# Second parts of weight tiles made by accumulating DMA instead of VectorE, and a room of its own for one sum

## The chip, the cores and the metric

The kernel runs on one core of one Trainium2 chip. The metric is the device time of one execution in microseconds. TensorE (PE) multiplies matrices, VectorE (DVE) and ScalarE (ACT) work on elements, GpSimd (POOL) does some elementwise work and issues DMAs, SyncE (SP) issues most loads. All matrix products of this kernel are float32 products made of three passes in a reduced float32 form ("fp32r"): every operand is split into a first part `hi`, the operand rounded to that form, and a second part `lo`, what the rounding left; the product is hi·hi + hi·lo + lo·hi.

## The reference

Two layers over 512 tokens of width 1024. Each layer is a half SwiGLU block, a mixing block, and another half SwiGLU block:

```python
x = x + 0.5 * swiglu(rms_norm(x, ffn1_norm[l]), ffn1_wg[l], ffn1_wu[l], ffn1_wd[l])
h = rms_norm(x, mix_norm[l])
z = h @ w_in[l]                       # 1024 x 2304: q | k | v | conv_B | conv_C | conv_h
attn_out = sliding_window_attention(q, k, v, attn_sink[l])   # 8 heads of 64, 2 of keys
conv_out = short_conv(z[B], z[C], z[H], conv_w[l])           # B * conv3(C * H), 3 taps
x = x + jnp.concatenate([attn_out, conv_out], axis=-1) @ w_out[l]
x = x + 0.5 * swiglu(rms_norm(x, ffn2_norm[l]), ffn2_wg[l], ffn2_wu[l], ffn2_wd[l])
```

A final RMS norm follows. The change is in the mixing block: the projection `h @ w_in` and the one by `w_out`.

## The kernel before

Activations are held transposed, with features on the 128 partitions and the 512 tokens along the row. Weights come from HBM in tiles of 128 x 1024 float32 values (512 KB).

**The stream of weight tiles.** `plan` writes the whole list of weight tiles (`order`) ahead of time, in the order in which TensorE takes them. For each it notes how the second part is made. `need_raw` loads tiles up to four ahead into eight buffers (`stock`, tag "raw"), by SP; a tile that is a sum of two weight blocks gets its second block by an accumulating DMA from POOL on top of the first (L193). The same eight buffers hold the attention's probabilities `p` and the values `vv`. `need_split` makes the two parts two tiles ahead, in three buffers each (`wh`, `wl`). There are two ways. `split` (L198, L199) lets ScalarE copy the tile to `hi` and VectorE subtract to get `lo`. `split_far` (L203 to L205) lets ScalarE write the negative of the tile, rounded, into `lo` and the copy into `hi`, and then an accumulating DMA issued by POOL adds the tile to `lo`. What `order` says is "far" goes the second way, all else the first.

**The input projection.** 18 tiles per layer, in the order of `MIX_COLS` (two tiles for each entry): keys, values, four tiles of queries, then for each half of the convolution's channels two tiles of C, two of H, two of B. `group` multiplies one tile with all 512 tokens: 24 matmuls of 512 columns, 5.4 us. Between the groups `mix` puts the attention, eight blocks (4 blocks of tokens by 2 groups of heads), each in three steps that `attend` spreads over the groups: `scores` (L1166, L1167; maxima and exponentials on VectorE and ScalarE, L1170 to L1195), `turn` (TensorE transposes the probabilities, L1202; ScalarE and VectorE split them, L1205 and L1206), and `values` (L1216, L1217; the result goes to `mixed[0]` by L1219 and L1222). The convolution of a channel tile is: product C·H on POOL (L1259), two scalings on ScalarE (L1261, L1263), one tap on VectorE (L1264), the sum on POOL (L1267), and the product with B into `mixed[1]` on POOL, or on VectorE for the last (L1274).

**The output projection.** `share` computes it by a scheme of seven products of quarter blocks in place of eight. The seven weight operands are named in `FORMS`: a11, a12, s2, s3, s1, a22, s4, each in two halves; s1 and s3 are the tiles loaded with an accumulating DMA, s2 and s4 are sums made in place (L223, L246). The seven activation operands are made by `Seven.make` from the four quarters b11, b12, b21, b22 of `mixed`: b11, b21 and b22 themselves, and t3 = b12 - b22, t2 = t3 - b11, t1 = b11 - b12, t4 = t2 + b21. All are split into two parts; t1, t4 and b22 by `split_far`. The sums t3 and t2 have a room of their own (`room_g8`); t1 is written over b12 and so has to come after t3:

```python
if what == "t1":
    nc.vector.tensor_sub(b12, b11, b12)
```

In the output projection the tile a11's first half gets its second part by `split_far`, the others by `split`.

**What orders the work.** A scheduler orders each engine's instructions when the program is built, outside of the stretch that is fixed by hand at the start. On the chip every engine works through its own list in order and waits by semaphores. A pool with n buffers makes a new tile wait until the oldest one's readers are done. A DMA's readers and writers are done when it has landed.

In trace names, `x_m`, `w_m`, `y_m` are the output projection's sums, `fb11h_m` and `fb11l_m` the parts of b11 (`ft2l_m`: second part of t2), `acc` the input projection's sums, `cb`, `cc`, `ch` the scaled convolution tiles B, C, H.

Of the kernel before, what the change touches and what calls it, by code (L numbers as in the profile page):

```python
# [8 lines left out]
F32 = mybir.dt.float32  # L9
# [6 lines left out]
P = 128  # L16
# [7 lines left out]
KC = D // P  # L24
# [3 lines left out]
H = S // 2  # L28
# [30 lines left out]
def trunk_kernel(  # L59
# [23 lines left out]
    nc = tc.nc  # L83
# [14 lines left out]
    def g8(name, dt=F32R, shape=(P, 2, 2, S)):  # L98
        return work.tile(list(shape), dt, tag="g8", bufs=4, name=name)
# [9 lines left out]
    def form(name, dt=F32R, shape=(P, KC // 2, H)):  # L109
        return xpool.tile(list(shape), dt, tag="xf", bufs=14, name=name)  # L110
# [57 lines left out]
    order = []  # L168
# [3 lines left out]
    def add_unit(*unit):  # L172
        units.append(unit)
        return len(units) - 1
# [109 lines left out]
    def abreast(kc):  # L284

        return max(1, KC // kc) if kc in (2, 4) else 1
# [10 lines left out]
    def plan():  # L297
        def cols(src, k0, kc, n, how=None):
            wide = abreast(kc)
            for b in range(0, n, wide):  # L300
                order.append((add_unit((src, k0, kc, b * P, wide * P)), how))

        def plain(wg, wu, b):
            for w in (wg, wu):
                for j in range(2):
                    order.append((add_unit((w, 0, KC, (2 * b + j) * P, P)), None))

        def up(wg, wu, b):
            top, low = ((w, k, KC // 2, 2 * b * P, 2 * P) for w, k in ((wu, 0), (wu, KC // 2)))
            first = (wg, 0, KC // 2, 2 * b * P, 2 * P)  # L310
            u = add_unit(first)
            add_unit((wg, KC // 2, KC // 2, 2 * b * P, 2 * P))
            add_unit(top, low)
            add_unit(top, first)
            add_unit(low)
            order.extend((u, what) for what in FORMS)

        def seven(at, how):


            u = len(units)
            for what in (((0, 0),), ((1, 0), (1, 1)), ((0, 1),), ((1, 0), (0, 0)), ((1, 1),)):
                for h in range(2):
                    add_unit(*(at(o, j, h) for o, j in what))
            order.extend((u, (what, h, how(what, h))) for what in FORMS for h in range(2))

        def ffn(wg, wu, wd, stages):
            for what, b in stages:
                how = "far" if b == (0,) and stages is not FIRST else None
                if what == "p":  # L330
                    plain(wg, wu, b)
                if what == "u":
                    up(wg, wu, b)
                if what == "w":
                    seven(
                        lambda o, j, h: ((wg, wu)[o], KC // 2 * j + 2 * h, 2, 2 * b * P, S),
                        lambda what, h: "far" if (b, what, h) == (1, "a11", 0) else None,
                    )
                if what == "s":
                    seven(  # L340
                        lambda o, j, h: (wd, 2 * b + KC // 2 * j + 2 * h, 2, o * S, S),
                        lambda what, h: "share",
                    )
                if what != "d":
                    continue
                if stages is not LAST or b[-1] < FF // (2 * P) - 1:
                    cols(wd, 2 * b[0], 2 * len(b), KC, how)
                    continue
                for half in range(2):
                    for k in range(0, 2 * len(b), 2):  # L350
                        u = add_unit((wd, 2 * b[0] + k, 2, half * S, S))
                        if half == 0:
                            order.append((u, "wide"))

        for l in range(DEPTH):
            ffn(ffn1_wg[l], ffn1_wu[l], ffn1_wd[l], INNER if l else FIRST)
            for c in MIX_COLS:
                for j in range(2):
                    order.append((add_unit((w_in[l], 0, KC, (2 * c + j) * P, P)), None))
            seven(  # L360
                lambda o, j, h: (w_out[l], KC // 2 * j + 2 * h, 2, o * S, S),
                lambda what, h: "far" if (what, h) == ("a11", 0) else "share",
            )
            ffn(ffn2_wg[l], ffn2_wu[l], ffn2_wd[l], INNER if l + 1 < DEPTH else LAST)


    MIX_COLS = (2, 0, 1, 5, 7, 3, 6, 8, 4)
    plan()


# [12 lines left out]
    class Norm:  # L383
        def __init__(self, i):
            self.i = i
            self.h = [None] * KC
            self.acc = None
            self.inv = None
            self.pairs = {}
            self.begun = set()  # L390
            self.order = range(KC)
# [100 lines left out]
    class Seven:  # L492

        def __init__(self, full, room, name, far=()):
            self.full, self.room, self.name, self.forms = full, room, name, {}
            self.far = far

        def make(self, *names):  # L500
            for what in names:
                if what in self.forms:
                    continue
                hi, lo = (form(f"f{what}{n}_{self.name}") for n in "hl")
                self.forms[what] = (hi, lo)
                b11, b12, b21, b22 = (
                    self.full[j][:, :, t * H : (t + 1) * H] for j in range(2) for t in range(2)
                )
                if what == "t2":
                    self.sums = self.room(self.name)  # L510
                    t3, t2 = self.sums
                    nc.vector.tensor_sub(t3, b12, b22)
                    nc.vector.tensor_sub(t2, t3, b11)
                if what == "t1":
                    nc.vector.tensor_sub(b12, b11, b12)
                if what == "t4":
                    nc.vector.tensor_add(self.sums[1], self.sums[1], b21)
                src = {"b11": b11, "b21": b21, "b22": b22, "t1": b12}.get(what)
                if src is None:
                    src = self.sums[0 if what == "t3" else 1]  # L520
                (split_far if what in self.far else split)(hi, lo, src)

    def room_g8(name):
        t = g8(f"sums_{name}", F32, (P, 2, KC // 2, H))
        return t[:, 0], t[:, 1]

    def room_stock(name):
        return [stock(f"sum{n}_{name}", shape=(P, KC // 2, H)) for n in range(2)]
# [577 lines left out]
    def mix(l, norm, after):  # L1106
        q = [None] * NH

        mixed = [g8(f"m_{l}_{j}", F32, (P, KC // 2, S)) for j in range(2)]
        ops = Seven(mixed, room_g8, f"m_{l}", far=("t1", "t4", "b22"))  # L1110

        def scaled(acc, name, by=None):
            t = g2(name)
# [11 lines left out]
        for g in range(NKV):  # L1125
            own = slice(g * HD, (g + 1) * HD)
# [20 lines left out]
        class Unit:  # L1147


            def __init__(self, n, g):  # L1150
                self.n, self.g = n, g
                self.name = f"{l}_{n}_{g}"
                self.lo = 0 if n else P
# [95 lines left out]
        for pair in range(2):  # L1249
            cs = []  # L1250
            for j in range(2):
                cs.append(scaled(group(norm.h), f"cc_{l}_{pair}_{j}"))
                attend(step)
                step += 1
            ys = []
            for j in range(2):
                c = 2 * pair + j
                u = scaled(group(norm.h), f"ch_{l}_{pair}_{j}")
                nc.gpsimd.tensor_mul(u, u, cs[j])  # L1259
                y = cs[j]  # L1260
                nc.scalar.activation(y, u, AF.Copy, scale=conv_of(l, 2, c))  # L1261
                tap = g2(f"tap_{l}_{c}")
                nc.scalar.activation(tap[:, 1:], u[:, : S - 1], AF.Copy, scale=conv_of(l, 1, c))  # L1263
                nc.vector.scalar_tensor_tensor(  # L1264
                    tap[:, 2:], u[:, : S - 2], conv_of(l, 0, c), tap[:, 2:], op0=ALU.mult, op1=ALU.add
                )
                nc.gpsimd.tensor_add(y[:, 1:], y[:, 1:], tap[:, 1:])  # L1267
                ys.append(y)
                attend(step)
                step += 1  # L1270
            for j in range(2):
                b = scaled(group(norm.h), f"cb_{l}_{pair}_{j}")
                eng = nc.vector if pair and j else nc.gpsimd
                eng.tensor_mul(mixed[1][:, 2 * pair + j, :], b, ys[j])  # L1274
                attend(step)
                step += 1
                if step == 17:
                    ops.make("b11")
        ops.make("b21", "b22")
        share(ops, 1.0, after.step, soon={0: ("t2", "t1"), 1: ("t3", "t4")})  # L1280

    class into:

# [53 lines left out]
```

## Time and profile before

| | us |
|---|---|
| median of 3 runs (lowest, highest) | 1692.32 (1690.91, 1693.9) |
| the profiled execution's own time | 1691.7 |
| its span, from first to last instruction | 1689.9 |
| TensorE busy | 1677.1 (99%) |
| VectorE busy | 1382.9 (82%) |
| ScalarE busy | 967.6 (57%) |
| GpSimd busy | 215.2 (13%) |
| granted TensorE clock | 0.999 |

A busy TensorE is not a TensorE at its peak: matmuls overlap and their ends are modelled, so gaps between them are read from their starts. In a run of 512-column matmuls one starts 0.23 us after the other, though each is shown as 0.39 us long. Layer 0's mixing block lies between about 349 and 513 us of the span, layer 1's between 1184 and 1347. The output projection starts at 470.5 and 1304.8.

### The profile page before, as it was taken

The numbers are of one execution on the slowest core, as the hardware profiler recorded it, in microseconds if no ns is written. First come the engines' busy times: TensorE is split into PE (matmuls) and PEld (weight loads), VectorE is DVE, ScalarE is ACT, GpSimd is POOL, SyncE is SP. The second block draws the span as 40 slices with busy tenths as digits, with TensorE's granted clock in tenths as the row PEclk, the third lists the DMA queues.
The fourth block names the chain that finished last, engine by engine and source line by source line (L and its number), as shares of the span: only waits on it lengthen the run. The fifth ranks groups of instructions, "written<-read, shape, count | busy, mean of one in ns | idle before, by whom it ended". The sixth has DMA issues, their size and how long they took to land.

```text
span 1689.9 us, 23565 instructions
## 1 busy us (share of the span) xinstructions
PE 1677.1 (99%) x9014; PEld 1443.9 (85%) x9014; DVE 1382.9 (82%) x1817; ACT 967.6 (57%) x1335; POOL 215.2 (13%) x192
## 2 busy tenths in 40 slices
PE   9999999999999999999999999999999999999998
PEld 7888899988898888889988888999888978888886
DVE  7987679988799876799798677997787998667995
ACT  6545565466566655564465555644555766556654
POOL 1011111001221111111011111110013111111111
PEclk9999999999999999999999999999999999999999
DMA  8467777731597677778566777884226867777881
GB/s 250 103 171 189 185 198 189 187 100 51 134 215 163 170 191 184 185 194 214 159 145 179 187 185 183 199 213 142 62 63 146 217 136 194 184 184 186 225 212 51
DMA packets 191846, 284.19 MB, mean 168 GB/s; under 512 B 9004, under 2 KB 77684, under 8 KB 191732
## 3 DMA queue, kind: packets, MB, share of 16 engines
q1 hardware_dynamic: 151108, 199.95, 37.4%
q0 software_dynamic: 39472, 81.27, 28.3%
q8 instruction: 71, 1.16, 0.3%
q10 hardware_dynamic: 1152, 1.45, 0.2%
q14 instruction: 43, 0.35, 0.1%
HBM read 261.14 MB, written 2.10 MB: 156 GB/s over the span
## 4 chain that ended last, share of the span: by engine, by line
PE 94%; DVE 2%; DMA 2%; issue 1%; POOL 0%; ACT 0%; POOLq 0%; DVEq 0%; SPq 0%; ACTq 0%
PE x L692 24%; PE y L692 12%; PE x_s L677 8%; PE acc L274 7%; PE acc L271 7%; PE acc L278 7%; PE w L692 6%; PE y_s L677 4%; PE x_s L692 3%; PE w_s L677 2%; PE x_m L677 2%; PE at L898 2%; DMA wl<-raw 2%; PE y_m L677 1%; PE y_s L692 1%
## 5 line engine op out<-in xcount | busy, mean ns | idle before, releaser
L198 ACT CAST wh<-raw 128x1024 fp32r<-128x1024 f32 (+1 forms) x482 | 505.2, 1048 | 536.8 <-PE x L692 133.9
L199 DVE TENSOR_TENSOR wl<-raw,wh 128x1024 fp32r<-128x1024 f32 (+1 forms) x481 | 588.5, 1226 | 206.8 <-ACT wh L198 204.9
L271 PE MATMUL acc<-xh,wh 128*128 128x512 f32 x448 | 176.6, 394 | 0.1
L274 PE MATMUL acc<-xl,wh 128*128 128x512 f32 x448 | 175.4, 392 | 0.1
L278 PE MATMUL acc<-xh,wl 128*128 128x512 f32 x416 | 162.5, 391 | 0.0
L193 POOL DMA_DIRECT2D raw<-in_ffn_wu_dram x39 | 47.2, 1216 | 530.2 <-DVE wl L199 252.7
L274 PEld LDWEIGHTS acc<-xl,wh 128*128 128x128 f32 x448 | 84.2, 188 | 18.5 <-DVE xl L402 1.5
L271 PEld LDWEIGHTS acc<-xh,wh 128*128 128x128 f32 x448 | 84.3, 188 | 17.5 <-ACT xh L401 0.5
L278 PEld LDWEIGHTS acc<-xh,wl 128*128 128x128 f32 x416 | 78.1, 188 | 16.1
L223 DVE TENSOR_TENSOR raw<-raw,raw 128x1024 f32<-128x1024 f32 x58 | 71.0, 1229 | 9.2 <-DMA wl<-raw 6.9
L193 POOL DMA_DIRECT2D raw<-in_ffn_wg_dram x39 | 47.3, 1249 | 229.2 <-DMA raw<-in_ffn_wu_dram 97.2
L193 POOL DMA_DIRECT2D raw<-in_ffn_wd_dram x32 | 38.6, 1210 | 259.4 <-DMA raw<-in_ffn_wd_dram 133.4
L692 PE MATMUL w<-wh,fb21h 128*128 128x512 f32 x152 | 60.7, 399 | 0.0
L692 PE MATMUL x<-wh,ft2h 128*128 128x512 f32 x152 | 60.6, 398 | 0.0
L692 PE MATMUL y<-wh,ft3h 128*128 128x512 f32 x152 | 60.4, 398 | 0.0
L692 PE MATMUL x<-wl,fb11h 128*128 128x512 f32 x152 | 59.3, 390 | 0.4 <-DMA wl<-raw 0.4
L692 PE MATMUL w<-wl,fb21h 128*128 128x512 f32 x152 | 59.4, 391 | 0.0
L692 PE MATMUL x<-wl,ft2h 128*128 128x512 f32 x152 | 59.3, 390 | 0.0
L692 PE MATMUL y<-wh,ft3l 128*128 128x512 f32 x152 | 59.2, 390 | 0.0
L692 PE MATMUL y<-wl,ft3h 128*128 128x512 f32 x152 | 59.2, 390 | 0.0
L692 PE MATMUL w<-wh,fb21l 128*128 128x512 f32 x152 | 59.2, 389 | 0.0
L692 PE MATMUL x<-wh,fb11l 128*128 128x512 f32 x152 | 59.1, 389 | 0.0
(497 smaller groups left out, 4807.4 us busy)
## 6 DMA issues: line engine op xcount, KB each, us to landing
raw<-in_ffn_wu_dram SPq DMA_DIRECT2D x127, 512.0 KB, 4.2
raw<-in_ffn_wd_dram SPq DMA_DIRECT2D x104, 512.0 KB, 4.9
raw<-in_ffn_wg_dram SPq DMA_DIRECT2D x87, 512.0 KB, 4.9
raw<-in_ffn_wu_dram POOLq DMA_DIRECT2D x39, 512.0 KB, 8.0
raw<-in_ffn_wg_dram POOLq DMA_DIRECT2D x39, 512.0 KB, 5.9
raw<-in_w_in_dram SPq DMA_DIRECT2D x36, 512.0 KB, 3.6
raw<-in_ffn_wd_dram POOLq DMA_DIRECT2D x32, 512.0 KB, 8.1
raw<-raw POOLq DMA_DIRECT2D x20, 512.0 KB, 7.0
```

Of the source, the lines that this page charges most:

```text
L193: nc.gpsimd.dma_start(out=r, in_=rows_of(*more), accum_op=ALU.add)
L198: nc.scalar.copy(hi, raw)
L199: eng.tensor_sub(lo, raw, f32(hi))
L223: nc.vector.tensor_add(a11, a11, s1)
L271: nc.tensor.matmul(acc, hi[:, k, :], rhs[k][0], start=k == first, stop=False)
L274: nc.tensor.matmul(acc, hi[:, k, :], rhs[k][1], start=False, stop=n == 0 and k == last)
L278: nc.tensor.matmul(acc, lo[:, k, :], rhs[k][0], start=False, stop=k == last)
L677: nc.tensor.matmul(accs[c // 2][:, c % 2, :], w[:, k, cols], x_[:, 2 * h + k, :], start=start and c % 2 == 0 and h + k + i == 0, stop=h + ...
L692: nc.tensor.matmul(accs[u], x_[:, 2 * h + k, tok], w[:, k, :], start=start and h + k + i == 0, stop=h + k == 2 and i == 2, skip_group_chec ...
L898: nc.tensor.transpose(tp[:, t * P : (t + 1) * P], ups[t][:, c * P : (c + 1) * P], ident)
```

## The change

Three edits, which act in both layers.

The last four entries of `MIX_COLS` (eight of the 18 tiles: the second channel half of C, H and B and the first half's B) are marked "far", so that their second parts are made by `split_far`. In the order of the stream these are tiles 11 to 18: first half's B, then C, H and B of the second half.

The output projection's first tile (a11, first half) loses the mark and is split by ScalarE and VectorE.

The sum t1 of the output projection gets a buffer of its own (the fourth of the four of tag "g8") instead of b12's place. So it no longer has to follow t3, and is asked for with b11 at step 17, ahead of b21 and b22.

```diff
-            for c in MIX_COLS:
+            for i, c in enumerate(MIX_COLS):
                 for j in range(2):
-                    order.append((add_unit((w_in[l], 0, KC, (2 * c + j) * P, P)), None))
+                    u = add_unit((w_in[l], 0, KC, (2 * c + j) * P, P))
+                    order.append((u, "far" if i >= MIX_FAR else None))
             seven(
                 lambda o, j, h: (w_out[l], KC // 2 * j + 2 * h, 2, o * S, S),
-                lambda what, h: "far" if (what, h) == ("a11", 0) else "share",
+                lambda what, h: "share",
             )
...
     MIX_COLS = (2, 0, 1, 5, 7, 3, 6, 8, 4)
+
+    MIX_FAR = 5
...
-        def __init__(self, full, room, name, far=()):
+        def __init__(self, full, room, name, far=(), own=None):
             self.full, self.room, self.name, self.forms = full, room, name, {}
-            self.far = far
+            self.far, self.own = far, own
...
                 if what == "t1":
-                    nc.vector.tensor_sub(b12, b11, b12)
+                    t1 = self.own(self.name) if self.own else b12
+                    nc.vector.tensor_sub(t1, b11, b12)
...
+    def room_one(name):
+        return g8(f"sum1_{name}", F32, (P, 2, KC // 2, H))[:, 0]
...
-        ops = Seven(mixed, room_g8, f"m_{l}", far=("t1", "t4", "b22"))
+        ops = Seven(mixed, room_g8, f"m_{l}", ("t1", "t4", "b22"), room_one)
...
                 if step == 17:
-                    ops.make("b11")
+                    ops.make("b11", "t1")
         ops.make("b21", "b22")
-        share(ops, 1.0, after.step, soon={0: ("t2", "t1"), 1: ("t3", "t4")})
+        share(ops, 1.0, after.step, soon={0: ("t2",), 1: ("t3", "t4")})
```

More of the change, by code (lines that the diff above doesn't have):

```diff
@@ L514, in make @@
                 if what == "t1":
-                    nc.vector.tensor_sub(b12, b11, b12)
+                    t1 = self.own(self.name) if self.own else b12
+                    nc.vector.tensor_sub(t1, b11, b12)
                 if what == "t4":
                     nc.vector.tensor_add(self.sums[1], self.sums[1], b21)
-                src = {"b11": b11, "b21": b21, "b22": b22, "t1": b12}.get(what)
-                if src is None:
+                src = {"b11": b11, "b21": b21, "b22": b22}.get(what)
+                if what == "t1":
+                    src = t1
+                elif src is None:
                     src = self.sums[0 if what == "t3" else 1]
```

## The prediction, made before the changed kernel was run

> **What bounds the kernel now.** I read the page first, then the stretches of the mixing stage by engine, then who made TensorE wait, then TensorE's and VectorE's rows at those places, and last the chain of waits through the end of layer 0's input projection. The page:
>
> ```profile
> span 1689.9 us, 23565 instructions
> PE 1677.1 (99%) x9014; PEld 1443.9 (85%) x9014; DVE 1382.9 (82%) x1817; ACT 967.6 (57%) x1335; POOL 215.2 (13%) x192
> ...
> PE 94%; DVE 2%; DMA 2%; issue 1%; POOL 0%; ACT 0%; POOLq 0%; DVEq 0%; SPq 0%; ACTq 0%
> ```
>
> TensorE sets the time. An edit that removes none of its instructions can only win the gaps between them. Two stretches of layer 0 (the last input tiles with their attention; the output projection):
>
> ```profile
> 420.00:470.00 50.00, 49.29 (x247) 41.37 (x246) 38.15 (x90) 26.13 (x55) 13.96 (x12) 1.00 0.52 128
> 470.00:513.00 43.00, 41.61 (x341) 41.05 (x341) 42.40 (x59) 30.80 (x42) 7.88 (x7) 1.00 0.90 208
> ```
>
> The columns are PE, PEld, DVE, ACT, POOL busy, granted clock, DMA share, GB/s. The clock is full. VectorE is nearly full from 470 on, ScalarE about half busy, the DMA engines half busy up to 470. The waits of TensorE over the whole run:
>
> ```profile
> PE o L1217 <- DVE pl L1206: 1.4, 2, 0.7
> PE w_m L677 <- DVE fb21l_m L199: 1.3, 2, 0.9
> PE x_m L677 <- DVE wl L199: 1.0, 2, 0.5
> ```
>
> So VectorE makes TensorE late at three places, once in each layer, and all three lie in the stage that is edited. The rows show the size, from start to start:
>
> ```profile
> 456.41 0.39 PE L1216 MATMUL o<-ph,vv 128*128 128x512 f32 x1
> 457.50 0.50 PE L1217 MATMUL o<-pl,vv 128*128 128x512 f32 x1 [0.71 <-DVE pl L1206]
> ...
> 476.27 0.28 PE L677 MATMUL w_m<-fb21h_m,wh 128*128 128x256 f32 x1
> 477.43 0.39 PE L677 MATMUL w_m<-fb21l_m,wh 128*128 128x256 f32 x1 [0.88 <-DVE fb21l_m L199]
> ...
> 483.52 0.28 PE L677 MATMUL x_m<-ft2l_m,wh 128*128 128x256 f32 x1
> 484.31 0.39 PE L677 MATMUL x_m<-ft2h_m,wl 128*128 128x256 f32 x1 [0.51 <-DVE wl L199]
> ```
>
> A 512-column matmul follows its forerunner by 0.23 us, a 256-column one by 0.12. The losses are 0.86 (call it gap 1), 1.04 (gap 2) and 0.67 (gap 3); the same rows of layer 1 give 0.81, 0.57 and 0.66. Layer 0 loses 2.57, layer 1 2.04, together **4.6 us. That is all the change can win** (0.27%). Gap 1 has its cause in VectorE's rows: the split of P18 takes 1.97 us beside a POOL sum and ends just before the part that TensorE waits for.
>
> ```profile
> 454.88 1.97 DVE L199 TENSOR_TENSOR wl<-raw,wh 128x1024 fp32r<-128x1024 f32 x1
> 456.77 0.68 DVE L1206 TENSOR_TENSOR pl<-pt,ph 128x512 fp32r<-128x512 f32 x1
> ```
>
> **The change, part by part (layer 0; layer 1 is the same 834 us later).** I call the 18 tiles of the input projection P1 to P18 and use the order of the built program.
>
> VectorE loses eight splits (P11 to P18), gets back the split of the first tile of the output projection: net seven of 1.14 us (start to start), 8.0 us per layer. Nearly all lie in its slack; only P18's lies on gap 1. With it gone the row at 456.77 can start when ScalarE's copy of the same block is there, at 455.3, and gap 1 goes (0.86). The sum t1 keeps its 1.22 us but moves from behind the second sum to a place before P18's scaling, where VectorE now idles: before, it sat 3.7 us until 467.36 on the landing of the one DMA-made tile, which the change makes by VectorE. So gap 3, where t1 stood ahead of the awaited split, goes (0.67, less than t1's 1.14).
>
> ScalarE gets net seven operations of 0.95 us (start to start of such rows), 6.7 us per layer, mostly in idle time (26.13 busy of 50). They stand ahead of attention copies at three places; the nearest is P18's at about 450.6, in the 1.39 us that it idles before the row at 451.95. Cost nothing; without that idle time it would be up to 0.95 at gap 1.
>
> POOL gets net seven DMA issues of 0.9 us and the DMA engines seven more 512 KB accumulations. Issue to landing of the 17 such transfers is 4.5 to 11.2 us, median 6.8: 6.2 beside one plain load (532), 8.0 at 459.35. P11 to P15 have their tiles 4 to 9 us before TensorE needs them, by 6.8. The cover there is the three-deep buffer of second parts; if it were gone each microsecond would be TensorE's.
>
> The new waits decide. A tile's raw buffer is freed by the landing of its accumulation now, so the first loads of the output projection wait for it on SP, and POOL, which works in order, waits for those loads before it adds to them. Before, the same place reads so in the chain of waits:
>
> ```profile
> 448.34 3.85 DMA raw<-in_w_out_dram
> 452.35 0.86 issue
> 453.21 1.22 POOL raw L193
> ...
> 458.13 1.22 POOL ch L1259
> 459.35 7.99 DMA wl<-raw
> ```
>
> The load is that of the second half of the sum s1, released by P17's split on VectorE. After: ScalarE has P17's negative at 444.4 (P14 ends at 442.3, then two operations), POOL issues at 444.8; landing 6.2 later (one load beside it) 451.0; SP's load 3.85: 455.0; POOL starts 0.9 after it: 455.9, instead of 453.21. Queued behind on POOL: P18's accumulation at 457.0, the convolution sum (1.3, ends 459.2) and the next product (1.3, ends 460.5, instead of 459.41). From that product's end to the last attention part, VectorE's second row of L1206 in that block, took 4.3 us (459.41 to 463.71), so 464.8; TensorE wants it at 464.85 less 0.86 = 464.0. **Late by 0.8**, where there was no gap. P18's part lands at 457.0 + 6.9 = 463.9 (between 6.2 and 7.6), needed at 464.7: in time.
>
> It also holds SP: the load of a12's second half waits for P18's landing, the one of s3 behind it starts at 464.5 and lands at 469.0 (4.5); POOL adds to it from 469.6 for 1.2, and only then makes the convolution product (1.4 to 2.1) that gap 2's operand comes from: 472.5. Then sum t3, a split and that split, 3.5 in all: 476.0; TensorE wants it at 476.27 - 0.86 + 0.12 = 475.5, so late by 0.5. Delays on one engine do not add, the later counts: 0.8 in place of gaps 1 and 2. Bounds of this lateness: 0 when landings take 4.5 (the quickest row), 5.4 when they take 8.0 (below). I take 0.8, as the nearest rows are those beside one load.
>
> The Trainium skill, "DMA: Bandwidth & Descriptors", section "Anatomy of one DMA", prices a POOL-issued DMA at 2.0 us plus bytes over 436 GB/s; 512 KB would take an estimated 3.2 us. By it the lateness would be 0 and the time that of rival A. The trace does not agree: no accumulation lands in under 4.4 us.
>
> Sum: layer 0 wins 2.57 - 0.8 = 1.8, layer 1 2.04 - 0.8 = 1.2, together 3.0. The profiled run took 1691.7 (1689.9 span plus 1.8 around it), 0.6 under the median 1692.3. So 1688.7 for it, **1689.3 us as the median**.
>
> **The rivals.** *A, all gaps go and none comes:* 1692.3 - 4.6 = 1687.7. For it: up to 470 the DMA engines have room, and accumulations with little beside them took 4.5 to 5.5 (862, 1360). Against: in the new order each has a load beside it.
>
> *B, the forecast;* its own range, by lateness 0 to 1.8, is 1688 to 1691.5.
>
> *C, the POOL and SP chain becomes the bound:* accumulations take 8.0 as at 459.35, the s1 load 4.35 (465.27), three loads in a row 6.3 (484.32). Then P17 lands at 452.8, load 457.3, POOL 458.2, P18 issued 459.3, landed 467.3, s3's load 474.2, POOL's product 477.4, gap 2's operand 480.9: late by 5.4. Twice that less 4.6 is +6.2: 1698.5. It turns the sign at a lateness of 2.3 (half of 4.6) and costs over 0.2% from 4.0. For it: every link is in series and shares the 16 engines, whose share from 420 to 470 rises from 0.52 to about 0.8 (28.3% of the span over some 155 POOL transfers is 3.1 us each, five more of them). Against: the loads before 459 landed in 3.8 to 4.3.
>
> The skill's same page, section "Issuing engines are not separate DMA queues", has all queues interleave on the same 16 engines; the rows agree (4.5 with one neighbour, 11.2 with three at 1370).
>
> *D, the edit does not reach the gaps,* since other work takes the freed slots: 1692.3. The order of the built program speaks against it.
>
> **How the numbers follow.** Chances: A 0.25, B 0.40, C 0.30, D 0.05. 0.2% (3.4 us) is about what a measurement of this kernel can tell from no change. Faster by more: A and a quarter of B (lateness under 0.6), 0.34. Within: the rest of B and D, 0.36. Slower: C, 0.30. As both signs hold much, B's own range stands above; mine runs from A less 0.7 (half the runs' spread to a side) to C: 1687.0 to 1699.0.
>
> **What would show it.** Right: no wait of TensorE for VectorE's P18 split, nor at gap 3; a new wait of about 0.8 at the last attention block's product (L1216 and L1217 rows near 464), POOL's accumulating load near 456, P18's landing near 464. A: no TensorE wait over 0.3 us in the stage. C: TensorE waits for a DMA-made tile or, near 477, for over 3 us. Wrong outright: waits before P16, or in other stages.

## The result and the profile after

The changed kernel takes **1695.57 us** (median; 1693.67 to 1698.92), the kernel before 1691.93 (1690.42 to 1693.90): the ratio is 1.0025, 95% interval 1.0019 to 1.0032. It is slower by 3.6 us, where the prediction said faster by 3.0. The profiled execution took 1698.92 (span 1697.0), 3.3 over the median, so what it lost has to be told apart from what every run loses. Lines from `Seven` on stand 9 lower in this kernel: L1206 is now L1215, L1216 and L1217 are L1225 and L1226, L677 is L686.

The page after, then the two stretches that the prediction showed (PE, PEld, DVE, ACT, POOL busy, granted clock, DMA share, GB/s):

```profile
span 1697.0 us, 23595 instructions
PE 1678.1 (99%) x9014; PEld 1444.5 (85%) x9014; DVE 1373.3 (81%) x1803; ACT 980.9 (58%) x1349; POOL 224.3 (13%) x206
...
PE 94%; DVE 2%; DMA 2%; issue 1%; ACT 1%; POOL 0%; SPq 0%; DVEq 0%; POOLq 0%; ACTq 0%
```

```profile
420.00:470.00 50.00, 47.39 (x236) 39.18 (x235) 33.13 (x87) 31.38 (x67) 14.49 (x14) 1.00 0.64 140
470.00:513.00 43.00, 42.02 (x334) 41.12 (x333) 40.86 (x54) 29.64 (x41) 8.55 (x8) 1.00 0.94 233
```

The edit did what it says: 14 VectorE instructions fewer, 14 more on ScalarE and on POOL. From 420 to 470 VectorE has 5 us less to do. TensorE shows 1.9 us less as well, because it stood. Who made TensorE wait (total, times, longest):

```profile
PE x L701 <- DMA wl<-raw: 2.1, 1, 2.1
PE o L1225 <- ACT ph L1214: 2.0, 1, 2.0
PE o L1226 <- DVE pl L1215: 1.8, 2, 1.2
PE pt L1211 <- DVE p L1204: 1.8, 2, 0.9
PE w_m L686 <- DVE fb21l_m L199: 1.6, 2, 1.0
```

Gap 3 is gone, and no attention block before the last waits. Gap 2 (`w_m`) stayed. Two waits are new in the stage: `pt`, once per layer, and the last attention block (`o`). One lies elsewhere: `x` L701, at 885, in layer 1's first half block. TensorE's rows of layer 0 at the three places:

```profile
406.12 0.28 PE L1175 MATMUL sc<-kh,q 128*128 128x256 f32 x1
407.29 0.87 PE L1211 MATMUL pt<-ident,p 128*128 128x128 f32 x6 [0.89 <-DVE p L1204]
...
464.00 0.39 PE L278 MATMUL acc<-xh,wl 128*128 128x512 f32 x1
466.38 0.49 PE L1225 MATMUL o<-ph,vv 128*128 128x512 f32 x1 [1.99 <-ACT ph L1214]
467.49 0.50 PE L1226 MATMUL o<-pl,vv 128*128 128x512 f32 x1 [0.62 <-DVE pl L1215]
...
480.90 0.39 PE L686 MATMUL w_m<-fb21l_m,wh 128*128 128x256 f32 x1 [0.98 <-DVE fb21l_m L199]
```

From start to start, less the usual 0.12 or 0.23, that is 1.05 at 406; 2.14 and 0.88 and two steps of 0.1 near 464, together 3.2; 1.14 at 480. Layer 1 has 1.05, 1.5 and 0.78. So the stage loses 5.4 and 3.3 where it lost 2.57 and 2.04: 4.1 more.

The stages, from TensorE's starts: *A* runs from the layer's first scores to the first `x_m`, *B* from there to the first `x` matmul of the second half block.

| | A, layer 0 | B, layer 0 | A, layer 1 | B, layer 1 | sum against before |
|---|---|---|---|---|---|
| before | 87.25 | 76.37 | 87.20 | 75.87 | |
| after | 90.49 | 75.72 | 88.69 | 75.36 | +3.6 |
| after, a second execution | 91.10 | 74.45 | 90.89 | 74.47 | +4.2 |

The +3.6 is also the difference of the medians. The rest of this execution's +7.1 lies for the most part (+4.05) between layer 0's second half block and layer 1's first scores, with the wait at 885 in it; in the second execution that stretch is as long as before (670.70 against 670.72), and its time was 1695.42. So the loss is made in the mixing stages, and the wait at 885 is there in one execution and not in the other.

### The profile page after: what moved, and what is told of

Its sections match the earlier page's. It is cut to its first block, busy times and chain, and to the rows that moved or that the text cites. A ratio compares the mean times of both kernels' runs of the same rounds, so it can differ in the third digit from the quotient of the medians.

```text
span 1697.0 us, 23595 instructions
## 1 busy us (share of the span) xinstructions
PE 1678.1 (99%) x9014; PEld 1444.5 (85%) x9014; DVE 1373.3 (81%) x1803; ACT 980.9 (58%) x1349; POOL 224.3 (13%) x206
## 3 DMA queue, kind: packets, MB, share of 16 engines
q8 instruction: 71, 1.16, 0.3%
q10 hardware_dynamic: 1152, 1.45, 0.2%
## 4 chain that ended last, share of the span: by engine, by line
PE 94%; DVE 2%; DMA 2%; issue 1%; ACT 1%; POOL 0%; SPq 0%; DVEq 0%; POOLq 0%; ACTq 0%
PE x L701 24%; PE y L701 12%; PE x_s L686 8%; PE acc L274 7%; PE acc L271 7%; PE acc L278 7%; PE w L701 6%; PE y_s L686 4%; PE x_s L701 3%; PE x_m L686 2%; PE w_s L686 2%; PE at L907 2%; PE y_m L686 1%; PE y_s L701 1%; DMA wl<-raw 1%
## 5 line engine op out<-in xcount | busy, mean ns | idle before, releaser
L198 ACT CAST wh<-raw 128x1024 fp32r<-128x1024 f32 (+1 forms) x468 | 490.5, 1048 | 517.7 <-PE x L701 136.1
L199 DVE TENSOR_TENSOR wl<-raw,wh 128x1024 fp32r<-128x1024 f32 (+1 forms) x467 | 571.3, 1225 | 211.0 <-ACT wh L198 209.5
L701 PE MATMUL x<-wl,fb11h 128*128 128x512 f32 x152 | 59.9, 394 | 2.1 <-DMA wl<-raw 2.1
L701 PE MATMUL w<-wh,fb21h 128*128 128x512 f32 x152 | 60.7, 399 | 0.0
L701 PE MATMUL x<-wh,ft2h 128*128 128x512 f32 x152 | 60.6, 398 | 0.0
L701 PE MATMUL y<-wh,ft3h 128*128 128x512 f32 x152 | 60.4, 398 | 0.0
L701 PE MATMUL x<-wh,fb11l 128*128 128x512 f32 x152 | 59.9, 394 | 0.0
L701 PE MATMUL w<-wl,fb21h 128*128 128x512 f32 x152 | 59.4, 391 | 0.0
L701 PE MATMUL x<-wh,fb11h 128*128 128x512 f32 x152 | 59.4, 393 | 0.0
L701 PE MATMUL x<-wl,ft2h 128*128 128x512 f32 x152 | 59.3, 390 | 0.0
L701 PE MATMUL y<-wh,ft3l 128*128 128x512 f32 x152 | 59.2, 390 | 0.0
L701 PE MATMUL y<-wl,ft3h 128*128 128x512 f32 x152 | 59.2, 390 | 0.0
```

Of the source, the lines that this page charges most:

```text
L198: nc.scalar.copy(hi, raw)
L199: eng.tensor_sub(lo, raw, f32(hi))
L701: nc.tensor.matmul(accs[u], x_[:, 2 * h + k, tok], w[:, k, :], start=start and h + k + i == 0, stop=h + k == 2 and i == 2, skip_group_chec ...
```

## The experiments

The edits below are to the line that sets the marks, `order.append((u, "far" if ... else None))`, unless another is shown; tile Pn has `2 * i + j == n - 1`. Each ratio is to the kernel before, run beside it, with its 95% interval. The kernel before had medians from 1691.02 to 1691.93 in these sets of runs, so where two kernels of different sets are compared, the difference is also given by what each is against its own run of before.

### Which part costs

**P11's mark away** (`"far" if 2 * i + j > 10`).

> Changed kernel, but tile P11 is split by VectorE again (P12 to P18 stay far). Built so, TensorE's order has the eight transposes of block (2,0) behind seven matmuls of P10's group again, as before the change. Theory T (two causes: the mark on P11 moves those transposes ahead, about 1.05 us of waiting per layer at the row near 406; the chain of P17 and P18 costs the rest): the wait for the normalised probabilities goes, the wait near 464 stays at 3.2 in layer 0; 1695.6 - 2.1 = 1693.5. Rival R1 (the chain alone): 1695.6. Rival R2 (every accumulation costs alike, 3.6 / 8 = 0.45 each): 1695.1.

1694.35, ratio 1.0018 (1.0009 to 1.0028): 1.2 less than the changed kernel, which alone is within the intervals. The wait for `p` is gone from its trace, as the built order says. The wait at 464, which theory T kept in layer 0, is not in this trace either: here the convolution's earlier product stood behind POOL's accumulating load (451.99), and the attention block before the last waited, four times between 456 and 458, 2.0 in all.

**P17's and P18's marks away** (`"far" if i in (5, 6, 7)`).

> Changed kernel, but tiles P17 and P18 are split by VectorE again (P11 to P16 stay far). TensorE's order is that of the changed kernel. Theory T: the wait near 464 (3.2 in layer 0, 1.5 in layer 1) goes and the wait for VectorE's split of P18 comes back (0.86 and 0.81): 1695.6 - 3.0 = 1692.6; the wait near 406 stays at 1.05. R1: the same 1692.6. R2: 1695.6 - 0.9 = 1694.7, with a wait near 464 still there.

1688.74, ratio 0.9980 (0.9972 to 0.9989): 6.8 less than the changed kernel, more than twice what theory T gave. The marks on these two tiles turn a gain into a loss. Of the stage's waits only the one for `p` is left, 0.9 per layer. Gap 1 did not come back, though VectorE splits P18 again. The split now stands at 454.31, ahead of both rows of L1215, with nothing of POOL beside it:

```profile
454.31 1.21 DVE L199 TENSOR_TENSOR wl<-raw,wh 128x1024 fp32r<-128x1024 f32 x1
```

**Both away** (`"far" if 10 < 2 * i + j < 16`: only P12 to P16).

> Changed kernel, but P11, P17 and P18 are split by VectorE again (only P12 to P16 far). Theory T: neither wait; gap 1 back, gap 3 gone: 1691.9 - 1.3 = 1690.6. R1: also 1690.6 if P11's mark costs nothing, but then the first of these four kernels would not be faster than the changed one. R2: 1695.6 - 1.35 = 1694.2.

1687.62, ratio 0.9976 (0.9967 to 0.9985). Theory T was 3 too high, R1 too (P11's mark does cost: 1.1 here against the one before). R2 fell: five marks gain.

**No mark** (`"far" if i >= 9`), with t1's room and a11 split by VectorE.

> Changed kernel without any far mark: the input tiles are split by VectorE as before, the sum t1 keeps its own room and a11's first half is split by VectorE. Theory T: as the one before, 1690.6, gap 1 present, gap 3 gone. R2: 1695.6 - 3.6 = 1692.0. A third rival, R3 (t1's new place and a11's split on VectorE cost something): above 1692.5.

1689.93, ratio 0.9989 (0.9981 to 0.9998), 0.7 under theory T; R3 fell. So the marks P12 to P16 are worth 2.3; they take gap 1 down (0.86 and 0.62 in this trace, 0.4 and none with them).

### What t1's room and a11's mark do

**t1's room alone** (kernel before, `Seven(..., room_one)`, `ops.make("b11", "t1")`, the new `soon`).

> Kernel before with the sum t1 in its own room, made with b11, and nothing else (no input tile far; a11's first half still far). With a11 split by VectorE as well, it was 1689.93, gaps 2 and 3 gone. Theory V (gap 3 was t1's place, gap 2 was VectorE standing until 467.4 for a11's landing before it may overwrite that tile): gap 2 stays, 1690.6. Rival (t1's place made both gaps): 1689.9, no wait of the w_m rows.

1695.55, ratio 1.0025 (1.0014 to 1.0035): worse than either theory. Gap 2 grew and got a second part:

```profile
PE w_m L686 <- DVE fb21l_m L199: 2.1, 2, 1.1
PE w_m L686 <- ACT fb21h_m L198: 1.3, 2, 0.7
```

With a11 still far, VectorE stands until 466.87, and t1 (1.21, at 471.98) then lies in the backlog, ahead of what gap 2 needs. The stage table gives +2.6 for the profiled execution (the quickest of this kernel's runs); the rest of the 4.5 is not seen in it.

**a11's mark away, alone** (kernel before, `lambda what, h: "share"`).

> Kernel before with the output projection's first tile split by VectorE, and nothing else. t1's room alone was slower than before by 4.5, both together faster by 2. Theory V (VectorE stands until about 467 for that tile's landing before it may overwrite it, all its later work is late by that): gap 2 goes, gap 3 stays or shrinks, 1689 to 1690.6. Rival (the two edits only work together): 1691 to 1692.

1688.96, ratio 0.9979 (0.9970 to 0.9988), no wait at gaps 2 and 3; gap 1 is left (1.4 in two). Theory V holds, and further than said: with VectorE's standing for a11's landing both gaps are gone. In the kernel before it stood 3.7 us there:

```profile
467.36 1.23 DVE L223 TENSOR_TENSOR raw<-raw,raw 128x1024 f32<-128x1024 f32 x1 [3.66 <-DMA wl<-raw]
```

**P12 to P16 without t1's room** (the mark as in the third; t1 as before).

> P12 to P16 far and a11 split by VectorE, but the sum t1 over b12 and after t3, as before the change. The same with t1's room was 1687.62. If t1's room wins gap 3 (0.67 and 0.66): 1688.9. If it wins nothing once VectorE no longer stands for a11's landing: 1687.6.

1687.15, ratio 0.9971 (0.9961 to 0.9981). t1's room brings nothing: without it the time is 0.5 less here and 1.0 less without marks, neither beyond the intervals. **This kernel has the lowest time of all**, 4.6 under its run of before, though the intervals do not tell it from P12 to P16 with t1's room; no wait of the mixing stage in its list is left.

**P12 to P15** (`"far" if 10 < 2 * i + j < 15`, with t1's room).

> Changed kernel with P12 to P15 far only. T1 says of P16 what it says of P17: its landing sets the start of the load under s1's first half. With P12 to P16 far POOL stands 10.9 us for that load, until 449.4, but the convolution's product behind it has its other operand only near then, and no later wait of TensorE follows. So T1: within 0.5 of 1687.62, to either side; with one split more on VectorE, up to 0.4 slower at gap 1.

1687.66, ratio 0.9972 (0.9960 to 0.9983): P16's mark is worth nothing measurable either way.

### Why P17 and P18 cost

**P17 alone, P18 alone**, beside P12 to P16 (`10 < 2 * i + j < 17`; `2 * i + j in (11, 12, 13, 14, 15, 17)`).

> Changed kernel with P12 to P17 far, P11 and P18 split by VectorE. The marks on P17 and P18 together cost 6.7 (1694.35 with both, 1687.62 with neither). Theory T1 (P17's landing sets the start of the load under s1's second half, for which POOL stands still with the convolution's work behind it): most of it comes with P17 alone, 1692 to 1694. Rival R4 (P18's own accumulation, issued late on POOL ahead of the convolution's sums and landing late, is what costs): 1687.6 to 1688.5.

> Changed kernel with P12 to P16 and P18 far, P11 and P17 split by VectorE. T1: the load under s1's second half starts again when VectorE has split P17, as before the change; P18's accumulation adds one issue of about 0.9 on POOL, and P18's split leaves VectorE: 1687 to 1689. R4: 1692 to 1694.

1691.95 (ratio 1.0007, 0.9998 to 1.0015) and 1688.31 (0.9985, 0.9977 to 0.9994). P17 costs most, as T1 says: 4.3 by the times, 5.2 by each kernel's own run of before. P18 alone costs 0.7 or 1.6 in the same way, which the intervals do not tell from nothing; the two together cost 6.7. POOL's rows with P17 far:

```profile
458.06 1.21 POOL L193 DMA_DIRECT2D raw<-in_w_out_dram  x1 [5.47 <-DMA raw<-in_w_out_dram]
458.84 1.74 POOL L1276 TENSOR_TENSOR cc<-cc,tap 128x511 f32<-128x511 f32 x1
460.09 1.74 POOL L1268 TENSOR_TENSOR ch<-ch,cc 128x512 f32<-128x512 f32 x1
```

**A ninth raw buffer** (tag "raw" 9 in place of 8, tag "g2" 12 in place of 14), with P12 to P18, P12 to P16, P12 to P17, and P12 to P16 with P18:

> The kernel of the first experiment (P12 to P18 far), with nine raw buffers in place of eight, so that each tile's load waits for the tile one earlier; for room the pool of 2 KB tiles (g2) has 12 in place of 14. The number of accumulations and their bytes stay. T1: the load under s1's second half waits for P16's landing, which was about 7 us before P17's, and POOL no longer stands still: 1687 to 1689.5, with no wait over 1 us near 456 and 464. R4, or rival R5 (more bytes on the 16 DMA engines slow every transfer): 1694, as with eight buffers.

> The kernel with nine raw buffers and twelve g2 buffers, but with P17 and P18 split by VectorE (P12 to P16 far). With nine buffers and P12 to P18 far it was 1695.29, although its trace shows no wait at 464. T1: with the ninth buffer the marks on P17 and P18 cost little more, so that this kernel is within 1.5 of it, 1693.8 to 1696.5; what is lost there is the price of the ninth buffer and the smaller pool in other stages. R4 and R5 (the accumulations themselves cost): 6.7 less, about 1688.6, as with eight buffers.

> Nine raw buffers, P12 to P17 far. With eight buffers P17's mark cost 4.3. T1 (it costs by the wait for its landing alone): near the nine-buffer kernel without it, 1689 to 1691. If the accumulation itself costs: 1693.5 or more.

> Nine raw buffers, P12 to P16 and P18 far. Theory W (P18's landing holds SP's next loads, POOL stands for s3's base load with the last convolution sum and product behind it, and these stretch VectorE's sums): wait at gap 2 of 1.0 to 1.8 per layer, stage of the attention unchanged; 1692 to 1695. If P17 and P18 cost only together: within 1 of 1689.9.

| nine buffers | time | ratio |
|---|---|---|
| P12 to P16 | 1689.90 | 0.9985 (0.9976 to 0.9995) |
| P12 to P17 | 1700.80 | 1.0057 (1.0045 to 1.0069) |
| P12 to P16 and P18 | 1693.79 | 1.0013 (1.0004 to 1.0022) |
| P12 to P18 | 1695.29 | 1.0028 (1.0017 to 1.0040) |

T1 as worded, the wait for P17's landing, fell: with that wait gone the marks still cost 5.4, and P17 alone 10.9 (6.2 and 11.7 by each kernel's own run of before; the kernel with P12 to P18 spread from 1691.05 to 1701.96). These times also fit the rivals by which the accumulations themselves cost. The scheduler wrote POOL's list anew. In the worst of these kernels POOL stood for another load, that of s3's first half, and again the convolution's product was queued behind it. That load started at 454.65, when VectorE had split P18, and took 6.60, so it did not wait for P17's landing:

```profile
461.54 1.20 POOL L193 DMA_DIRECT2D raw<-in_w_out_dram  x1 [4.88 <-DMA raw<-in_w_out_dram]
462.31 1.74 POOL L1268 TENSOR_TENSOR ch<-ch,cc 128x512 f32<-128x512 f32 x1
...
466.69 0.49 PE L1225 MATMUL o<-ph,vv 128*128 128x512 f32 x1 [3.22 <-ACT ph L1214]
```

With P18 alone stage A is untouched and gap 2 pays, as theory W has it (1.16 and 1.45 from start to start in a row in layer 0, 1.20 in layer 1).

**The product moved**, POOL's standing left as it is:

```diff
-                nc.gpsimd.tensor_mul(u, u, cs[j])
+                (nc.vector if pair and j else nc.gpsimd).tensor_mul(u, u, cs[j])
```

with P11 to P18, P12 to P17 and P12 to P16:

> The changed kernel with the product C*H of the last channel tile on VectorE in place of POOL. POOL's list is otherwise the same, and so are all loads and accumulations. Theory Q (what costs is that product, queued on POOL behind the load under s1's second half; ScalarE's two scalings and the copy of the last attention block queue behind it): the wait near 464 goes in both layers (2.7 to 3.2 and 1.4 to 1.5), the waits at P10 (1.05 per layer) stay: 1691 to 1692. Rival (the transfers cost, or POOL's standing delays TensorE in another way): 1695 to 1696.

> P12 to P17 far, same product on VectorE. With it on POOL 1691.95. Theory Q: P17's mark then costs little, 1687 to 1688.5, no wait near 463. Rival: 1691.5 to 1692.5.

> P12 to P16 far, same product on VectorE: the control. With it on POOL 1687.62. Both theories: 1687 to 1688.2; VectorE has 0.7 more per layer, and one stretch by POOL less.

With P12 to P17: 1688.84 (ratio 0.9981, 0.9972 to 0.9990); the control 1688.72 (0.9979, 0.9970 to 0.9988). **P17's mark costs 0.1 here; with the product on POOL it cost 4.3** (5.2 by each kernel's own run of before). In the mixing stages of the profiled executions it costs 0.9 here and 4.5 there. The accumulations are the same, so for this mark the rival that they cost falls. Both times lie above the ranges given, by 0.3 and 0.5, and one wait is left near 464 in layer 0 (0.96, for VectorE). POOL still stands for the load, 4.77 instead of 5.47, but only a sum is behind it:

```profile
457.21 1.21 POOL L193 DMA_DIRECT2D raw<-in_w_out_dram  x1 [4.77 <-DMA raw<-in_w_out_dram]
457.99 1.75 POOL L1276 TENSOR_TENSOR cc<-cc,tap 128x511 f32<-128x511 f32 x1
```

The whole change with the product moved did not follow: 1695.48 (ratio 1.0020, 1.0011 to 1.0029), where theory Q gave 1691 to 1692. The wait near 464 did not go either: 1.2 is left in layer 0 and 1.05 in layer 1, now for VectorE. Its sum of two weight tiles, beside POOL's late convolution sum, took three times its 1.22 in layer 0, and the moved product 3.01 instead of 0.69 in layer 1. TensorE also waits for P18's landing itself (467.20), and gap 2 has 2.4 in two:

```profile
PE w_m L686 <- DVE fb21l_m L199: 2.4, 2, 1.5
PE o L1226 <- DVE pl L1215: 1.9, 2, 1.0
...
PE acc L278 <- DMA wl<-raw: 0.4, 1, 0.4
...
459.34 3.69 DVE L223 TENSOR_TENSOR raw<-raw,raw 128x1024 f32<-128x1024 f32 x1
459.83 2.10 POOL L1276 TENSOR_TENSOR cc<-cc,tap 128x511 f32<-128x511 f32 x1
```

**The changed kernel once more:**

> The changed kernel once more, as it is. If the mixing stages hold the whole difference, they take about 3.6 more than before again (3.24 + 1.49 in the input projections, -0.65 - 0.51 in the output projections), with waits at P10, near 464 and at gap 2; the wait in layer 1's first half block (2.1) is there or not by chance, and the time is 1694 to 1699 accordingly.

1695.42 in a single run, with waits at P10 and near 464 in both layers, none at 885 and, other than expected, none at gap 2: TensorE came to it later, 3.7 to 3.9 late out of stage A, so its operand was there.

## Why the prediction was wrong, step by step

The parts, each from a pair of runs, taken against its own run of before where the two are of different sets: a11's mark away -2.8, t1's room +0.9, marks P12 to P16 -2.3, P17 and P18 +6.7, P11 +1.2; together +3.7 against +3.6 measured. That they meet is so by construction; their sizes are the answer. (Each ratio is good to about 1.5 us: P11's cost rests on two pairs and the trace, t1's is not told from nothing.)

The forecast left 1.6 us of waits in the two layers; the profiled execution has 8.7. Three steps failed, in order of size: the decisive chain (4.7 instead of 1.6), P11's mark, put at nothing (2.1), and gap 2, taken as covered by the chain (1.9). The stated range held the measured time only because it reached up to rival C; its middle was on the other side.

- **"What it can win is 4.6": right**, and all of it can be had: the kernel with the lowest time wins 4.6. But two of the three gaps had another cause than I worked with. I saw VectorE stand 3.7 us for a11's landing and counted it only as t1's place. The line that takes a11's mark away wins gaps 2 and 3 by itself; t1's room, which I credited with gap 3, wins nothing.
- **Gap 1 goes because P18's split leaves VectorE: not the needed part.** With P12 to P16 alone it nearly goes, though VectorE still splits P18.
- **"P11 to P15 have their tiles in time": right, and their cost of nothing was still wrong for P11.** The tile lands early (403.64), but its mark alters TensorE's order: six transposes of block (2,0) were put ahead of P10's matmuls, and there VectorE's normalisation is not done: 1.05 per layer. The order of the built program showed this before any run; I compared the engines that the edit touches and not TensorE.
- **"ScalarE: cost nothing": right** as far as seen; the wait for its copy at 464 comes from what is ahead of it, the scalings that wait for POOL's product.
- **The decisive chain: place right, size wrong. This is the largest step that failed.** In layer 0 P17 landed at 452.68 (said 451.0), the load under s1's second half at 458.46 (455.0; it took 5.73, not 3.85, with another load and POOL's accumulating load beside it), POOL began its accumulating load at 459.03 (455.9), the product ended at 463.7 (460.5), VectorE's last part at 467.4 (464.8). Lateness 3.2 in layer 0 and 1.5 in layer 1, not 0.8. The rows of layer 0, with the wait in brackets:

```profile
459.03 1.20 POOL L193 DMA_DIRECT2D raw<-in_w_out_dram  x1 [5.67 <-DMA raw<-in_w_out_dram]
459.79 1.38 POOL L205 DMA_DIRECT2D wl<-raw  x1
460.39 2.11 POOL L1276 TENSOR_TENSOR cc<-cc,tap 128x511 f32<-128x511 f32 x1
461.64 2.09 POOL L1268 TENSOR_TENSOR ch<-ch,cc 128x512 f32<-128x512 f32 x1
463.77 0.72 ACT L1270 ACTIVATE cc<-ch,par 128x512 f32<-128x512 f32 x1 [5.81 <-POOL ch L1268]
```

  The mis-sized terms: the landing by 0.9 (7.1 for 6.2), the load by 1.9, and ahead of them 0.8 of delay from the wait at 406. In layer 1 the errors nearly cancelled: P17 landed after 4.56, the load took 5.72, and POOL's product ended at 1302.1, only 0.6 later than the sum has it (stage A starts 841.0 later there). VectorE added the rest. Its split of a11's first half fell beside POOL's sum and product, took 4.26 instead of 1.22, and held the tap behind it until 1304.39, though ScalarE's part was there at 1303.5:

```profile
1298.95 4.26 DVE L199 TENSOR_TENSOR wl<-raw,wh 128x1024 fp32r<-128x1024 f32 x1 [0.21 <-ACT wh L198]
1303.25 1.23 DVE L223 TENSOR_TENSOR raw<-raw,raw 128x1024 f32<-128x1024 f32 x1
1304.39 0.74 DVE L1273 SCALAR_TENSOR_TENSOR tap<-ch,par,tap 128x510 f32<-128x510 f32 x1
```

  So what POOL does late reaches TensorE in two ways: through the product, by ScalarE, and through VectorE, which it holds up. Moving the product acts on both, and shows together what they cost with P17's mark. That the marks on P17 and P18 cost 6.7 in the whole change is shown as well; how this divides over the links there is read from these rows, and no edit shows it.
- **"P18 lands in time": wrong.** It landed at 467.83, 8.0 after its issue, said 463.9. The attention's wait hid it; with the product moved TensorE waits for it.
- **"Late by 0.5" at gap 2, and "the later counts":** s3's load landed at 473.59 (469.0) and the operand was 1.14 late *on top of* the 3.2. Delays on one engine do not add, but P18's landing moved with the first delay, so the second kept its distance. In the second execution it did not.
- **The rivals:** C had the chain (POOL's accumulating load at 458.2, measured 459.03), and its landing time of 8.0 is what P18 took. But it put its loss of 5.4 at gap 2, near 477, where 1.14 and 0.78 were measured; its sign, a TensorE wait of over 3 there, did not come, so its total of +6.2 was too much. What I set against it, that the loads before 459 landed in 3.8 to 4.3, was a misreading: in the same trace the load at 456.88 took 4.55 and the one at 458.91 took 8.27, with three and four transfers beside them. And the change itself adds transfers there. The Trainium skill, "DMA: Bandwidth & Descriptors", section "Issuing engines are not separate DMA queues", which has all queues interleave on the same engines, was quoted and then not used to size the load. The traces agree with it: with five transfers in flight in the nine-buffer kernel, landings took 10.6 to 12.0.
- **"Wrong outright: waits before P16 or in other stages":** the first came true at P10.
- **Small slips in the sums:** A and a quarter of B make 0.35, not 0.34, and a lateness of 0 to 1.8 gives B the range 1687.7 to 1691.3. The row at 532, taken as a landing beside one load (6.2), had two POOL transfers beside it as well towards its end. None of these alters the forecast's sign.

## What to carry to other kernels

When work moves to a queue that runs in order, list what stands behind each of its waits and look for the one entry that the critical engine needs: with P17's mark, moving that entry away was worth 4.2 us here. It can still fail to pay, as in the whole change, where other waits took its place. Give the transfers that a change adds the landing times of a stretch as crowded as the one it makes, not those of today's quiet stretch. And compare the built order of every engine, the bound one first, even where the edit has nothing to do with it.

## What the runs showed of the hardware

VectorE and POOL hold each other up. In the trace of before, the one that starts first goes undisturbed: a split that starts 0.09 after a POOL product (414.19) takes 2.28, and the product its usual 1.28; a split that starts 0.24 ahead of a POOL product (469.11) takes 1.22, and the product 2.14. The some 580 splits of weight tiles and sums of two of them take 1.21 to 1.23 there, more than 100 of them beside a DMA issue of POOL, but for six that began while a POOL sum or product ran. The Trainium skill, "SBUF — State Buffer", section "Who interferes with whom", calls the port pair that the two share an exclusive lock, by which the later one fully blocks; these rows agree.

Other traces have rows that do not fit so simply. VectorE's operation began during a DMA issue of POOL and ahead of the POOL sum or product that followed, and was stretched all the same: 3.65 and 3.69 with nine buffers and with the product moved, 4.52 with P12 to P17 (458.40), 4.74 in the second execution of the changed kernel (459.18), all instead of 1.22. In others it was not, and POOL's operation was (464.50 with P12 to P16: 1.23, and POOL's 1.96 instead of 1.28). Which of the two it will be stays open. So an operation of POOL that is delayed can cost a second time, by what it then falls beside.

An accumulating transfer of 512 KB landed 4.4 after its issue with nothing beside it (P11, P13), 7.1 and 8.0 with one or two others under way (P17, P18), and 10.6 with four (P18 with nine buffers). It matters how much the neighbour still has to move: in layer 1 P17 landed after 4.6, beside a load that had begun 1.9 ahead of it; in layer 0 the load began 0.2 behind it, and yet from 446.6 to 449.2 that load's queue had 230 of the 238 packets.
